# Scoring the level of 32 of a gated recurrence with whole-array matmuls, by turning token blocks of 64 in place of 32

## The chip, the cores and the metric

The kernel runs on one core of a Trainium2 chip. The metric is the device time of one execution in microseconds (us), as a median of several runs. The engines are named as in the profile: PE is TensorE (its matmuls; PEld are its weight loads), DVE is VectorE, ACT is ScalarE, POOL is GpSimd and SP is SyncE.

## The reference

One decoder layer over 2,048 tokens of width 1,024, all in float32. The tokens are normalized and projected; four heads run an HGRN2 recurrence with a forget gate `f` per key channel, eight heads run sliding-window attention with sinks; both are projected back and added. A gated MLP with a short causal convolution and a last normalization follow. The change touches the recurrence, which the reference computes in chunks:

```python
b = jnp.cumsum(gi, axis=2)                                  # gi = log f
rel = b[:, :, :, None, :] - b[:, :, None, :, :]
decay = jnp.exp(jnp.where(causal, rel, -jnp.inf))
scores = jnp.einsum('bhtk,bhsk,bhtsk->bhts', qi, ki, decay)
intra = jnp.einsum('bhts,bhsv->bhtv', scores, vi)
inter = jnp.einsum('bhtk,bhkv->bhtv', qi * jnp.exp(b), state)
```

A score of query t against key s is a sum over 128 channels of q, k and the product of all gates between s and t. This product differs by channel, so the scores are not one plain matmul of q and k.

## The kernel before, in words

The sequence is worked in two halves of 1,024 tokens (`HALF`), each first through the mixer (`hgrn`, `attend`), then through `out_proj`, `gate_up` and `down`. Large products are made in a split form: every operand is a high and a low part (`hi`, `lo`, `XH`, `XL`), and three matmuls take the place of one. The four recurrence heads and four attention units of a half are generators; the list `ORDER` says in which order their stages are traced (`l3`, for example, is the stage of head 3 that holds the levels). The framework then plans every engine's order of instructions with a simulated timeline, so the order on the chip is an interleaving: between a level and the next one of a head, TensorE is given matmuls of other units (`pvv` of L630 to L632, `pop`, `q`, `g` of L218). Each engine runs its own list in order. The last head of a half has the first units of `out_proj` (`pop`) as its company; their operands `XL` are made by VectorE at L230.

The recurrence (`hgrn`) holds `K` and `Q` with the 128 key channels on the partitions and the 1,024 tokens in columns, eight chunks of 128 (`TT` = 8). It scores in levels m = 1, 2, 4, ..., 64 (`LEVELS`). At level m a chunk is cut into blocks of 2m tokens; the queries of the later half of each block are scored against the keys of its earlier half, an m x m tile of `ST` (keys on rows, queries in columns). Afterwards the later half's `Q` is multiplied by the gates' product over the earlier half and the earlier half's `K` by that over the later half (`F`, L523 and L524 or L534 and L535), and `F` is contracted to half its length (L538). So at each level the decay between a block's halves is already in `K` and `Q`.

Levels below 32 take two chunks at a time, u of the first 512 tokens and u + 4 of the second. To make that possible, the tokens of the second 512 are laid out in turned order within blocks of 32: the host permutes the columns of `xP` by `index ^ 31`, and `blocks(t, turn)` reads such columns backwards where true order is needed (L352, L374, L500, L607, L609). In a turned block the earlier half stands behind the later one. Thus the keys wanted from chunk u lie in the even blocks of m, those from chunk u + 4 in the odd ones. ScalarE gathers both into `G` (L515), 128 columns for each u; one matmul for each u (L517) has them as weights and the 2 x 64 queries as moving operand. Four such matmuls make 128 x 128 products each, of which the wanted tiles are a part; VectorE copies these into `ST` with `copy_predicated` under a mask `lmask` (L542). The masks are made by GpSimd in `constants` (L110 to L120).

Levels 32 and 64 are scored in plain slices: for 32, two blocks in each of eight chunks, 16 matmuls (L531) with 32 columns as weights and 32 moving columns; for 64, eight matmuls of 64 columns. ScalarE copies their products from PSUM to `ST`, for 32 in two copies (L552), for 64 in two (L548). The level products `plev` stand in a PSUM ring `hg` of two banks. A float32 matmul has two records in the trace, with a weight load for each.

Later stages read `ST` (L590), the final `K` (L564) and `Q` (L592).

Of the kernel before, what the change touches and what calls it, by code (L numbers as in the profile page):

```python
# [17 lines left out]
P = 128  # L18
D = 1024
KT = D // P  # L20
S = 2048
HALF = 1024
NH = S // HALF
TT = HALF // P
# [17 lines left out]
LEVELS = [1, 2, 4, 8, 16, 32, 64]  # L42
# [7 lines left out]
def hymba_layer(ctx: ExitStack, tc: tile.TileContext, a: dict, out: bass.AP, rows_out: bass.AP):  # L50
    nc = tc.nc
# [47 lines left out]
    def constants():  # L99

        C.own = cp.tile([P, P], F32, name="own")
        C.ownT = cp.tile([P, P], F32, name="ownT")
        C.prevT = cp.tile([P, P], F32, name="prevT")
        for t, op, sgn in ((C.own, ALU.is_ge, 1), (C.ownT, ALU.is_ge, -1), (C.prevT, ALU.is_gt, 1)):
            nc.gpsimd.memset(t, 1.0)
            nc.gpsimd.affine_select(out=t, in_=t, compare_op=op, fill=0.0, base=0,
                                    pattern=[[-sgn, P]], channel_multiplier=sgn)

        C.lmask = {}
        for m in LEVELS[:5]:  # L110
            t = cp.tile([P, 2, 64], F32, name=f"lmask{m}")
            nb = 64 // m
            nc.gpsimd.memset(t, 1.0)
            for side in range(2):
                ts = t[:, side]
                nc.gpsimd.affine_select(out=ts, in_=ts, compare_op=ALU.is_ge, fill=0.0, base=-side * m,
                                        pattern=[[-2 * m, nb], [0, m]], channel_multiplier=1)
                nc.gpsimd.affine_select(out=ts, in_=ts, compare_op=ALU.is_ge, fill=0.0, base=m - 1 + side * m,
                                        pattern=[[2 * m, nb], [0, m]], channel_multiplier=-1)
            C.lmask[m] = t  # L120

        battn = C.battn = cp.tile([P, 6], F32, name="battn")
        nc.sync.dma_start(battn, a["b_attn"])
        C.bq = cp.tile([P, ATT_J], F32, name="bq")
        nc.vector.tensor_scalar(C.bq, battn[:, 0:ATT_J], 0.125, None, op0=ALU.mult)
        C.hgw = cp.tile([P, 1], F32, name="hgw")
        nc.sync.dma_start(C.hgw, a["hg_norm_w"])
        nc.vector.tensor_scalar(C.hgw, C.hgw, 0.5, None, op0=ALU.mult)
        C.sinkb = cp.tile([P, ATT_J, 2], F32, name="sinkb")
        nc.sync.dma_start(C.sinkb.rearrange("p j k -> p (j k)"), a["sinks"].to_broadcast([P, 8]))  # L130
        C.nfw = cp.tile([P, KT], F32, name="nfw")
        nc.sync.dma_start(C.nfw, a["norm_ffn_w"])
        C.fnw = cp.tile([P, KT], F32, name="fnw")
        nc.sync.dma_start(C.fnw, a["final_norm_w"])
        C.cw = cp.tile([P, FT, 4], F32, name="cw")
        nc.sync.dma_start(C.cw, a["conv"])

        lbl = cp.tile([P, 2, HG], F32, name="lbl")
        nc.sync.dma_start(lbl, a["lb_logits"])
        lbm = cp.tile([P, HG], F32, name="lbm")  # L140
        nc.vector.tensor_tensor(lbm, lbl[:, 0], lbl[:, 1], op=ALU.max)
        lbe = cp.tile([P, 2, HG], F32, name="lbe")
        nc.vector.tensor_tensor(lbe, lbl, lbm.unsqueeze(1).to_broadcast([P, 2, HG]), op=ALU.subtract)
        nc.scalar.activation(lbe, lbe, AF.Exp)
        nc.vector.tensor_tensor(lbm, lbe[:, 0], lbe[:, 1], op=ALU.add)
        nc.vector.reciprocal(lbm, lbm)
        C.lb = cp.tile([P, HG], F32, name="lb")
        nc.vector.tensor_tensor(C.lb, lbe[:, 0], lbm, op=ALU.mult)
        C.omlb = cp.tile([P, HG], F32, name="omlb")
        nc.vector.tensor_scalar(C.omlb, C.lb, -0.5, 0.5, op0=ALU.mult, op1=ALU.add)  # L150
        nc.vector.tensor_scalar(C.lb, C.lb, 0.5, 0.5, op0=ALU.mult, op1=ALU.add)
# [172 lines left out]

    def blocks(t, turn=False):

        v = t.rearrange("p (g r) -> p g r", r=32)
        return v[:, :, ::-1] if turn else v

    def across(t, base, dims):  # L330
# [4 lines left out]
    def rows(kv):  # L335
        return slice(kv * HD, (kv + 1) * HD)
# [123 lines left out]
    def hgrn(hf, h, X, invb, vs, WG, gates, mix, p, fu=None):  # L460
# [13 lines left out]
        K = p.tile([P, HALF], F32, tag="K", name="K", bufs=2)  # L474
        nc.vector.tensor_scalar(K, f, -1.0, 1.0, op0=ALU.mult, op1=ALU.add)
        Q = p.tile([P, HALF], F32, tag="Q", name="Q", bufs=2)
# [3 lines left out]
        ST = p.tile([P, TT, P], F32, tag="t4", name="ST", bufs=2)  # L480
# [6 lines left out]
        for k in range(2):  # L487
            r = rows(k)
# [19 lines left out]
        for m in LEVELS:  # L508
            nb = HALF // (2 * m)
            pl = ps("hg", "plev")  # L510
            if m < 32:
                n, nu = 64 // m, TT // 2
                far, near = [[512 - m, 2], [P, nu], [2 * m, n], [1, m]], [[512 + m, 2], [P, nu], [2 * m, n], [1, m]]
                G = p.tile([P, 512], F32, tag="G", name="G", bufs=2)
                nc.scalar.copy(across(G, 0, [[m, 2], [P, nu], [2 * m, n], [1, m]]), across(K, 0, near))  # L515
                for u in range(nu):
                    marks[m] = nc.tensor.matmul(across(pl, u * 64, [[256, 2], [1, 64]]), G[:, u * P:(u + 1) * P],  # L517
                                                across(Q, u * P + m, [far[0]] + far[2:]), start=True, stop=True)
                nf = P // m
                Kv, Qv = across(K, 0, near), across(Q, m, far)  # L520
                Fk = across(F, 1, [[4 * nf - 1, 2], [nf, nu], [2, n], [0, m]])
                Fq = across(F, 0, [[4 * nf + 1, 2], [nf, nu], [2, n], [0, m]])
                nc.vector.tensor_tensor(Kv, Kv, Fk, op=ALU.mult)  # L523
                nc.vector.tensor_tensor(Qv, Qv, Fq, op=ALU.mult)  # L524
            else:
                Qv = Q.rearrange("p (b w m) -> p b w m", w=2, m=m)
                Kv = K.rearrange("p (b w m) -> p b w m", w=2, m=m)
                for c in range(TT):
                    for s0 in range(0, P, 2 * m):
                        o = pl[s0:s0 + m, c * m:(c + 1) * m] if m < 64 else pl[rows(c % 2), c // 2 * m:(c // 2 + 1) * m]  # L530
                        nc.tensor.matmul(o, K[:, c * P + s0:c * P + s0 + m],  # L531
                                         Q[:, c * P + s0 + m:c * P + s0 + 2 * m], start=True, stop=True)
                Fv = F.rearrange("p (b w) -> p b w", w=2)
                nc.vector.tensor_tensor(Qv[:, :, 1], Qv[:, :, 1], Fv[:, :, 0:1].to_broadcast([P, nb, m]), op=ALU.mult)  # L534
                nc.vector.tensor_tensor(Kv[:, :, 0], Kv[:, :, 0], Fv[:, :, 1:2].to_broadcast([P, nb, m]), op=ALU.mult)  # L535
            Fv = F.rearrange("p (b w) -> p b w", w=2)
            Fn = p.tile([P, max(nb, 16)], F32, tag=f"F{m}", name=f"F{m}", bufs=1)[:, 0:nb]
            nc.vector.tensor_tensor(Fn, Fv[:, :, 0], Fv[:, :, 1], op=ALU.mult)  # L538
            F = Fn
            if m < 32:  # L540
                mk = C.lmask[m].bitcast(U32).rearrange("p s t -> p (s t)")
                nc.vector.copy_predicated(across(ST.rearrange("p c t -> p (c t)"), m, far),  # L542
                                          across(mk, 0, [[64, 2], [0, nu], [m, n], [1, m]]),
                                          pl.rearrange("p (s u b m) -> p s u b m", s=2, u=nu, m=m))
                continue
            if m == 64:
                for k in range(2):
                    nc.scalar.copy(ST[0:m].rearrange("p (c k) t -> p c k t", k=2)[:, :, k, m:],  # L548
                                   pl[rows(k), 0:TT // 2 * m].rearrange("p (c m) -> p c m", m=m))
                continue  # L550
            for s0 in range(0, P, 2 * m):
                nc.scalar.copy(ST[s0:s0 + m, :, s0 + m:s0 + 2 * m],  # L552
                               pl[s0:s0 + m, 0:TT * m].rearrange("p (c m) -> p c m", c=TT))
        yield
        v = vs[h]

# [2 lines left out]
        for b in range(NB):  # L559
            pk = ps("hg", "pkn")  # L560
            n = min(4, kept - 4 * b)
            for i in range(n):
                c = slice((b * 4 + i) * P, (b * 4 + i + 1) * P)
# [17 lines left out]
        g = q  # L581
# [3 lines left out]
        for c in range(TT):  # L585
            cs = slice(c * P, (c + 1) * P)
            prev = state[:, h] if c == 0 else SS[:, c - 1]
            o = po[c // 4][:, c % 4 * P:(c % 4 + 1) * P]
# [512 lines left out]
    for hf in range(NH):  # L1101
        X, kv, invb, rs, f0 = nxt
        with ExitStack() as st:
            p = pool(f"mix{hf}", stack=st, reuse_waits="tile")
# [21 lines left out]
        with ExitStack() as st:  # L1126
            p = pool(f"ffn{hf}", stack=st, reuse_waits="tile")
# [5 lines left out]
def _layout(i):  # L1133
# [3 lines left out]
    def cols(w, idx):  # L1137
# [3 lines left out]
    x = i["x"][0]  # L1141
    w_in = i["w_in"][0]
    ar = np.arange
# [4 lines left out]
    rows = [ar(P) + h * P for h in range(4)]  # L1148
# [3 lines left out]
    conv = np.concatenate([i["conv_w"][0], i["conv_b"]], 0)  # L1152
    d = {
        "xT": x.T.reshape(KT, P, S),
        "xP": x[np.where(ar(S) // 512 % 2, ar(S) ^ 31, ar(S))].T.reshape(KT, P, S),
        "norm_mix_w": i["norm_mix_w"][0].reshape(KT, P).T,
        "w_q": np.stack([cols(w_in, h * P + ar(P)) for h in range(4)]),
        "w_f": np.stack([cols(w_in, 512 + h * P + ar(P)) for h in range(4)]),
# [41 lines left out]
```

## Time and profile before

| | before |
|---|---|
| median of 3 runs | 2150.42 us (2149.98 to 2150.78) |
| the profiled execution | 2150.84 us |
| its span | 2149.1 us |
| PE busy | 2130.8 us |
| DVE busy | 1630.1 us |
| ACT busy | 1020.0 us |

The span runs from the first instruction of the program to the last. Busy time is time in which the engine has an instruction under way; matmuls are pipelined and overlap, so PE's busy time says that work was there, and the steps between starts of matmuls say what it cost. In a row of the timeline, `x8` stands for eight instructions merged into one row, and `[0.62 <-DVE XL L230]` says that the engine had been idle 0.62 us before it, until DVE had done line 230. In the view of who waited for whom the numbers are the total, how often, and the longest.

### The profile page before, as it was taken

The numbers are of one execution on the slowest core, as the hardware profiler recorded it, in microseconds if no ns is written. First come the engines' busy times: TensorE is split into PE (matmuls) and PEld (weight loads), VectorE is DVE, ScalarE is ACT, GpSimd is POOL, SyncE is SP. The second block draws the span as 40 slices with busy tenths as digits, with TensorE's granted clock in tenths as the row PEclk, the third lists the DMA queues.
The fourth block names the chain that finished last, engine by engine and source line by source line (L and its number), as shares of the span: only waits on it lengthen the run. The fifth ranks groups of instructions, "written<-read, shape, count | busy, mean of one in ns | idle before, by whom it ended". The sixth has DMA issues, their size and how long they took to land.

```text
span 2149.1 us, 29229 instructions
## 1 busy us (share of the span) xinstructions
PE 2130.8 (99%) x11271; PEld 1790.8 (83%) x11271; DVE 1630.1 (76%) x2443; ACT 1020.0 (47%) x1818; POOL 19.8 (1%) x45
## 2 busy tenths in 40 slices
PE   8999999999999999999999999999999999999998
PEld 6988988888888888888889889888888888888887
DVE  6576768788887888785765767677988888787765
ACT  5445553564444435345634446535544344444453
POOL 2000000000000000000000000000000000000000
PEclk9999999999999999999999999999999999999999
DMA  4111012423232334974631011124233323259643
GB/s 158 40 30 40 31 30 79 137 65 124 92 123 88 103 118 152 370 251 148 214 138 40 30 31 32 40 75 158 69 103 103 118 84 122 95 183 399 238 147 133
DMA packets 91148, 254.41 MB, mean 118 GB/s; under 512 B 11137, under 2 KB 13953, under 8 KB 91009
## 3 DMA queue, kind: packets, MB, share of 16 engines
q1 hardware_dynamic: 90576, 252.29, 34.9%
q8 instruction: 88, 1.44, 0.3%
q14 instruction: 52, 0.42, 0.1%
q10 hardware_dynamic: 432, 0.27, 0.0%
HBM read 195.37 MB, written 57.15 MB: 117 GB/s over the span
## 4 chain that ended last, share of the span: by engine, by line
PE 93%; DVE 5%; ACT 1%; DMA 1%; issue 1%; SPq 0%; DVEq 0%; ACTq 0%
PE X L765 7%; PE X L763 7%; PE X L764 7%; PE pop L218 6%; PE q L218 4%; PE hq L218 4%; PE f L218 4%; PE Y L764 4%; PE Y L763 4%; PE Y L765 4%; PE pdx L950 3%; PE pdx L951 3%; PE pdx L952 3%; PE g L218 3%; PE pdy L950 3%; PE pdy L952 3%
## 5 line engine op out<-in xcount | busy, mean ns | idle before, releaser
L638 ACT CAST whi<-raw 128x1024 fp32r<-128x1024 f32 x88 | 92.7, 1053 | 115.5 <-PE X L764 71.2
L763 PE MATMUL X<-T,whi 128*128 128x512 f32 x352 | 136.9, 389 | 0.0
L764 PE MATMUL X<-T,whi 128*128 128x512 f32 x352 | 136.9, 389 | 0.0
L765 PE MATMUL X<-T,wlo 128*128 128x512 f32 x352 | 136.9, 389 | 0.0
L834 DVE SCALAR_TENSOR_TENSOR y<-ga,cw,y 128x1024 f32<-128x1024 f32 x88 | 112.5, 1278 | 25.9 <-ACT y L832 25.8
L639 DVE TENSOR_TENSOR wlo<-raw,whi 128x1024 fp32r<-128x1024 f32 x88 | 107.0, 1216 | 4.4 <-ACT whi L638 4.4
L769 ACT COPY u<-X 128x512 f32<-128x512 f32 x88 | 51.5, 585 | 122.1 <-PE X L765 121.9
L199 ACT CAST whi<-raw 128x1024 fp32r<-128x1024 f32 x58 | 60.5, 1048 | 98.5 <-issue 20.6
L639 DVE TENSOR_TENSOR xld<-raw,xhd 128x1024 fp32r<-128x1024 f32 x72 | 81.0, 1130 | 18.9 <-ACT xhd L638 18.6
L638 ACT CAST xhd<-raw 128x1024 fp32r<-128x1024 f32 x72 | 69.8, 978 | 40.2 <-DMA raw<-act0T 14.3
L218 PE MATMUL pop<-XL,whi 128*128 128x512 f32 x256 | 84.2, 392 | 0.9 <-DVE XL L230 0.9
L218 PE MATMUL pop<-XH,wlo 128*128 128x512 f32 x256 | 83.3, 391 | 0.7 <-DVE wlo L200 0.7
L218 PE MATMUL pop<-XH,whi 128*128 128x512 f32 x256 | 83.2, 396 | 0.8 <-ACT XH L229 0.5
L200 DVE TENSOR_TENSOR wlo<-raw,whi 128x1024 fp32r<-128x1024 f32 x58 | 70.4, 1217 | 12.9 <-ACT whi L199 12.9
L764 PEld LDWEIGHTS X<-T,whi 128*128 128x128 f32 x352 | 66.1, 188 | 13.7
L765 PEld LDWEIGHTS X<-T,wlo 128*128 128x128 f32 x352 | 66.1, 188 | 13.7
L763 PEld LDWEIGHTS X<-T,whi 128*128 128x128 f32 x352 | 66.1, 188 | 13.7
L630 PE MATMUL pvv<-whi,XH 128*128 128x256 f32 x256 | 73.0, 286 | 0.0
L631 PE MATMUL pvv<-whi,XL 128*128 128x256 f32 x256 | 72.9, 286 | 0.0
L632 PE MATMUL pvv<-wlo,XH 128*128 128x256 f32 x256 | 72.0, 285 | 0.0
L765 PE MATMUL X<-B,wlo 128*128 128x512 f32 x176 | 68.7, 390 | 0.8 <-DVE wlo L639 0.8
L763 PE MATMUL Z<-B,whi 128*128 128x512 f32 x176 | 68.7, 390 | 0.0
(390 smaller groups left out, 6396.5 us busy)
## 6 DMA issues: line engine op xcount, KB each, us to landing
wr<-in_w_down SPq DMA_DIRECT2D x90, 512.0 KB, 5.7
raw<-in_w_gate SPq DMA_DIRECT2D x44, 512.0 KB, 3.6
raw<-in_w_up SPq DMA_DIRECT2D x44, 512.0 KB, 3.6
raw<-act0T SPq DMA_DIRECT2D x20, 512.0 KB, 6.0
raw<-act1T SPq DMA_DIRECT2D x20, 512.0 KB, 5.5
act0B<-y SPq DMA_DIRECT2D x33, 256.0 KB, 2.3
act1B<-y SPq DMA_DIRECT2D x33, 256.0 KB, 2.4
raw<-in_w_out SPq DMA_DIRECT2D x16, 512.0 KB, 3.6
```

Of the source, the lines that this page charges most:

```text
L218: nc.tensor.matmul(o[b], w, x[:, bs], start=f, stop=l)
L630: nc.tensor.matmul(o[:, 0:256], xh[:, t], hi[:, c], start=kt == 0, stop=False)
L631: nc.tensor.matmul(o[:, 0:256], xl[:, t], hi[:, c], start=False, stop=False)
L632: nc.tensor.matmul(o[:, 0:256], xh[:, t], lo[:, c], start=False, stop=kt == KT - 1)
L638: nc.scalar.copy(h, src)
L639: return (eng or nc.vector).tensor_tensor(l, src, h.bitcast(F32), op=ALU.subtract)
L763: nc.tensor.matmul(o, wh[:, ws], xh, start=i == 0 and not more, stop=False, skip_group_check=more)
L764: nc.tensor.matmul(o, wh[:, ws], xl, start=False, stop=False, skip_group_check=more)
L765: nc.tensor.matmul(o, wl[:, ws], xh, start=False, stop=i == 3, skip_group_check=more)
L834: nc.vector.scalar_tensor_tensor(y, g[:, w:w + HALF], C.cw[:, ft, w:w + 1], y, op0=ALU.mult, op1=ALU.add)
L950: nc.tensor.matmul(o, wh[:, i, c], ah[:, i, cols], start=f, stop=False, skip_group_check=more)
L952: nc.tensor.matmul(o, wl[:, i, c], ah[:, i, cols], start=False, stop=l, skip_group_check=more)
```

## The change

Blocks of 64 are turned in place of 32, on the host and in `blocks`. The level of 32 goes over to the branch of the lower levels: a gather by ScalarE into `G`, four matmuls of 128 x 128, the two multiplications with that branch's access patterns, and a masked copy by VectorE with a sixth mask. The plain branch is left to level 64 alone, and the 16 narrow matmuls and two ScalarE copies of the level of 32 go.

```diff
         C.lmask = {}
-        for m in LEVELS[:5]:
+        for m in LEVELS[:6]:
             t = cp.tile([P, 2, 64], F32, name=f"lmask{m}")
...
-        v = t.rearrange("p (g r) -> p g r", r=32)
+        v = t.rearrange("p (g r) -> p g r", r=64)
         return v[:, :, ::-1] if turn else v
...
-            if m < 32:
+            if m < 64:
                 n, nu = 64 // m, TT // 2
...
                 for c in range(TT):
-                    for s0 in range(0, P, 2 * m):
-                        o = pl[s0:s0 + m, c * m:(c + 1) * m] if m < 64 else pl[rows(c % 2), c // 2 * m:(c // 2 + 1) * m]
-                        nc.tensor.matmul(o, K[:, c * P + s0:c * P + s0 + m],
-                                         Q[:, c * P + s0 + m:c * P + s0 + 2 * m], start=True, stop=True)
+                    o = pl[rows(c % 2), c // 2 * m:(c // 2 + 1) * m]
+                    nc.tensor.matmul(o, K[:, c * P:c * P + m], Q[:, c * P + m:(c + 1) * P], start=True, stop=True)
...
-            if m < 32:
+            if m < 64:
                 mk = C.lmask[m].bitcast(U32).rearrange("p s t -> p (s t)")
...
-            if m == 64:
-                for k in range(2):
-                    nc.scalar.copy(ST[0:m].rearrange("p (c k) t -> p c k t", k=2)[:, :, k, m:],
-                                   pl[rows(k), 0:TT // 2 * m].rearrange("p (c m) -> p c m", m=m))
-                continue
-            for s0 in range(0, P, 2 * m):
-                nc.scalar.copy(ST[s0:s0 + m, :, s0 + m:s0 + 2 * m],
-                               pl[s0:s0 + m, 0:TT * m].rearrange("p (c m) -> p c m", c=TT))
+            for k in range(2):
+                nc.scalar.copy(ST[0:m].rearrange("p (c k) t -> p c k t", k=2)[:, :, k, m:],
+                               pl[rows(k), 0:TT // 2 * m].rearrange("p (c m) -> p c m", m=m))
...
-        "xP": x[np.where(ar(S) // 512 % 2, ar(S) ^ 31, ar(S))].T.reshape(KT, P, S),
+        "xP": x[np.where(ar(S) // 512 % 2, ar(S) ^ 63, ar(S))].T.reshape(KT, P, S),
```

## Prediction

> **What bounds the kernel now.** I read the page's busy table and chain first, then TensorE's waits, then the timeline around single levels of the recurrence.
>
> ```profile
> span 2149.1 us, 29229 instructions
> PE 2130.8 (99%) x11271; PEld 1790.8 (83%) x11271; DVE 1630.1 (76%) x2443; ACT 1020.0 (47%) x1818; POOL 19.8 (1%) x45
> PE 93%; DVE 5%; ACT 1%; DMA 1%; issue 1%; SPq 0%; DVEq 0%; ACTq 0%
> ```
> ```profile
> PE kv L218 <- ACT XH L232: 6.0, 1, 6.0
> ...
> PE plev L517 <- DVE Q L524: 0.4, 1, 0.4
> ...
> PE kv L218 <- DVE XL L233: 0.2, 1, 0.2
> ```
>
> TensorE is busy 99% of the span and carries 93% of the chain that ended last. The second fence is the view of who TensorE waited for; it has ten rows, of which the first, one from the middle and the last are shown. They add up to 12.4 us, 6.0 of it at the very first unit. The levels' whole-array matmuls (plev, L517) wait 0.4 us in the whole kernel. So an edit of this recurrence is worth what it changes in TensorE's own time, unless its new steps on VectorE (DVE) or ScalarE (ACT) come so late that TensorE stands. I settle these two things in turn.
>
> **TensorE: 16 narrow matmuls go, 4 whole-array ones come, in each of eight heads** (four heads in each half of the sequence). The level of 16 already has the form that the level of 32 is to get, so one passage of each beside the same neighbours gives the price. In the timeline the columns are start, duration, engine, line; a float32 matmul has two records, so 16 are x32 and 4 are x8.
>
> ```profile
> 82.11 0.28 PE L632 MATMUL pvv<-wlo,XH 128*128 128x256 f32 x1
> 82.23 0.28 PE L630 MATMUL pvv<-whi,XH 128*128 128x256 f32 x1
> 82.24 0.98 PEld L517 LDWEIGHTS plev<-Q,G 128*128 128x128 f32 x8
> 82.36 1.06 PE L517 MATMUL plev<-Q,G 128*128 128x128 f32 x8
> 83.17 0.36 PE L631 MATMUL pvv<-whi,XL 128*128 128x256 f32 x1
> ...
> 86.36 0.28 PE L630 MATMUL pvv<-whi,XH 128*128 128x256 f32 x1
> 86.56 0.59 PEld L531 LDWEIGHTS plev<-Q,K 128*32 128x32 f32 x32
> 86.56 0.70 PE L531 MATMUL plev<-Q,K 128*32 128x32 f32 x32
> 87.19 0.39 PE L631 MATMUL pvv<-whi,XL 128*128 128x256 f32 x1
> ```
>
> Durations overlap, so only starts count. Two pvv matmuls follow each other by 82.23 - 82.11 = 0.12 us. With a whole-array level between them the step is 83.17 - 82.23 = 0.94, so that level costs 0.94 - 0.12 = 0.82 us. With the 16 narrow matmuls the step is 87.19 - 86.36 = 0.83, so the level of 32 costs 0.71 us today. This holds the wait on entry: the first narrow matmul starts 0.20 after its neighbour, against 0.12 to 0.13 for any other. A second passage, beside matmuls of 512 columns:
>
> ```profile
> 178.28 0.39 PE L218 MATMUL g<-XH,wlo 128*128 128x512 f32 x1
> 178.51 0.39 PE L218 MATMUL g<-XH,whi 128*128 128x512 f32 x1
> 178.83 0.70 PE L531 MATMUL plev<-Q,K 128*32 128x32 f32 x32
> 179.46 0.33 PE L399 MATMUL psc<-KS,qh 128*128 128x128 f32 x1
> ```
>
> Here it is 179.46 - 178.51 less the step of 0.23, or 0.72. The narrow matmuls are cheap because they run 0.59 / 32 = 0.018 us apart, where the wide ones run 0.98 / 8 = 0.12 apart. So a quarter as many matmuls are not a gain: the change adds 0.82 - 0.715, about 0.1 us, in each head. For the six heads whose levels lie in gapless TensorE work that is +0.6 us; the last head of each half I treat below.
>
> Why are the wide ones no faster? A 128x128 record and a 128x256 one both follow the one before by 0.12, half the columns for the same time, so their columns do not set the pace. The Trainium skill, "TensorE: Matmul & The Clock Gate", section "LDWEIGHTS (loading the stationary operand)", puts a load at its columns divided by 1.2 GHz. By it both forms load the same 1,024 columns (32 x 32 or 8 x 128), 0.85 us, and the change would be worth 0.0 on TensorE where the rows give +0.1 a head; the wide loads (0.98 us for eight) fit it roughly, the narrow ones (0.59 for 32) beat it, so I keep the rows.
>
> **VectorE gets a masked copy, ScalarE trades two copies for one.** The columns of a line's view are the shortest, median and longest duration in ns; the last row is of the view by groups.
>
> ```profile
> L542 DVE COPY_PREDICATED ST<-lmask,plev x40: 693/718/1341, 64.7 to 1416.7; 128x512 f32<-128x512 uint32 x40
> L515 ACT COPY G<-K x40: 606/622/697, 54.4 to 1408.7; 128x512 f32<-128x512 f32 x40
> L552 ACT COPY ST<-plev x16: 344/362/367, 87.3 to 1419.8; 32x256 f32<-32x256 f32 x16
> L118 POOL TENSOR_SCALAR_AFFINE_SELECT lmask<-lmask 128x64 f32<-128x64 f32 x10 | 7.9, 827 | 0.0
> ```
>
> ScalarE loses 2 x 0.36 and gains 0.62 a head: -0.1 us on an engine that is busy 47% of the time. VectorE gains one copy of 0.72 a head. The mask costs GpSimd one memset and four selects, two of them of this row, about 3 us at the start of the kernel; the first masked copy of all is at 64.7 us, so nothing waits. The turning of 64 tokens changes the stride of copies and products, and no counts. The host's permutation of x adds no DMA.
>
> Is VectorE's copy covered? Two stretches, first head and last head of the first half; the columns are length, then TensorE, weight loads, VectorE and ScalarE busy:
>
> ```profile
> 60.00:95.00 35.00, 35.00 (x325) 33.02 (x324) 18.92 (x29) 14.00 (x31) 0.00 (x0) 1.00 0.08 29
> 320.00:355.00 35.00, 33.88 (x250) 28.35 (x251) 34.86 (x52) 18.02 (x40) 0.00 (x0) 1.00 0.37 116
> ```
>
> In the first head VectorE idles 16 of 35 us and TensorE never: covered. In the last head VectorE is full (34.86 of 35) and TensorE misses 1.1 us: here an added 0.72 us would count, if it stands ahead of what TensorE waits for. The order of that stretch, VectorE first:
>
> ```profile
> 347.39 0.67 DVE L523 TENSOR_TENSOR K<-K,F 128x512 f32<-128x512 f32 x1
> ...
> 351.27 1.21 DVE L230 TENSOR_TENSOR XL<-hg,XH 128x1024 fp32r<-128x1024 f32 x1
> 352.40 0.69 DVE L534 TENSOR_TENSOR Q<-Q,F 128x512 f32<-128x512 f32 x1
> ...
> 358.95 0.69 DVE L534 TENSOR_TENSOR Q<-Q,F 128x512 f32<-128x512 f32 x1 [3.68 <-PE plev L531]
> ```
> ```profile
> 351.22 0.70 PE L531 MATMUL plev<-Q,K 128*32 128x32 f32 x32
> 352.54 0.73 PE L218 MATMUL pop<-XL,whi 128*128 128x512 f32 x2 [0.62 <-DVE XL L230]
> ...
> 1418.56 0.73 PE L218 MATMUL pop<-XL,whi 128*128 128x512 f32 x2 [0.31 <-DVE XL L230]
> ```
> ```profile
> 348.50 0.59 ACT L456 CAST XH<-poT 128x512 fp32r<-128x512 f32 x1 [5.05 <-PE poT L446]
> ```
>
> The multiplications themselves go over to the lower levels' access pattern (L523, 0.67 us, where L534 takes 0.69): no cost shows. TensorE waits for the split XL (L230), which starts at 351.27. The new masked copy can't run before the level's matmuls have ended, and they only start at 351.22, when XL is about to begin. So it comes behind XL, beside the multiplications at 352.40, and behind those VectorE is idle 3.68 us before the level of 64: covered. The new gather G needs K of the level of 16, done at 348.06; ScalarE has been idle for 5.05 us at 348.50, so it can gather then, and at most delays the cast there by 0.2. The level's longer TensorE time falls into the wait for XL. So these two heads cost between 0 and 0.8 each (0.1 + 0.72 if the copy did go first); I take 0.05, near the covered end, because the rows put XL ahead. What is late next there is XL itself, unchanged.
>
> Sum: 6 x 0.1 + 2 x 0.05 = +0.7 us on TensorE's path. The profiled execution took 2150.84 us (span 2149.1 and 1.7 around it), 0.4 over the median of 2150.42; the same step on the median gives 2151.1.
>
> **What the sum can't see: the order is planned anew.** The two halves of the sequence run the same code in slightly different orders.
>
> ```profile
> 1152.02 0.70 PE L531 MATMUL plev<-Q,K 128*32 128x32 f32 x32
> ```
>
> From the level of 32 in the first head to the pop matmul behind it in the last, the first half takes 352.54 - 86.56 = 265.98 us and the second 1418.56 - 1152.02 = 266.54. So a different order moves a half by about 0.6 us; two halves give some 1.2 us about the sum: 2150 to 2152.5.
>
> **The rivals.**
> *VectorE carries the levels (slower).* The copy sits on VectorE between a level and the next one's products in all heads, and TensorE stands for it each time: 8 x 0.72 = 5.8 for the copies and 8 x 0.1 for the matmuls: 2150.42 + 6.6 = 2157.0. For it: the full stretch at 320. Against it: the slack of 16 us in the first head and TensorE's 0.4 us of waits at L517. It decides from the point at which VectorE's queue is longer than the other matmuls set between two levels, which today is so in the last heads alone; a plan that spreads such filler differently could make it so elsewhere. Chance 0.12.
> *The new order drops waits (faster).* K's multiplication waits for the gather alone, where it waited for 16 matmuls; K then runs ahead. All waits but the first in the view of waits are 12.4 - 6.0 = 6.4 us; should a plan happen to lose them all, the time is 2150.42 + 0.8 - 6.4 = 2144.8; losing the two XL waits alone gives 2150.2. Most of the 6.4 lies in other stages, which the change doesn't touch. Chance 0.10, of which 0.05 by more than 4.3 us.
> *Wide matmuls at the pace of their columns.* A step of 0.23 for 512 columns is 0.057 for 128; eight would cost 0.46 where 16 narrow ones cost 0.71: -0.25 x 8 = -2.0, 2148.4. For it: nothing but that row. Against it: the eight records of the level of 16, 0.12 apart, the very form that is to come. Chance 0.03. The Trainium skill, same page, section "Back-to-back issue gap", gives 60 cycles for up to 64 columns and 134 for 128; at 2.4 GHz 32 records would take 0.80 us and 8 would take 0.45, an estimate of -0.35 a head and 2147.6 in all; the trace disagrees at both ends.
>
> **How the numbers follow.** About 0.2% (4.3 us) is what a measurement of this kernel can tell from no change. The forecast of 2151.1 has chance 0.75, and its own range, 2150 to 2152.5, lies inside that. Slower by more: the first rival, 0.12. Faster by more: 0.05. The rest, 0.83, is no change. For 8 in 10 I take the forecast's range, the loss of a few waits and the wide-column case below (2148), and above it the cost of both last heads' copies, the gather behind other ScalarE work and part of the first rival: 2155.
>
> **What would show it right or wrong.** Right: L531 has a third of its 384 records (128), L517 has 384, L542 and L515 have 48, L552's two copies are gone; the step around the level of 32 is 0.94 between pvv matmuls; VectorE's busy time is up by some 5 us and TensorE's by about 1; TensorE's waits stay near 12 us. Wrong: TensorE waits at L517 of a microsecond and more, or at XL in the last heads by over 1; an XL split behind the masked copy; wide records closer than 0.11 us.

## The result, and the profile after

| | before | after |
|---|---|---|
| median | 2150.22 us (2149.43 to 2151.00) | 2154.59 us (2153.93 to 2155.12) |
| the profiled execution | 2150.84 us | 2154.80 us |
| its span | 2149.1 us | 2153.1 us |

The ratio is 1.0020, 95% interval 1.0013 to 1.0027: the change costs 4.4 us where 0.7 were forecast. The time lies near the upper end of the predicted range, and the size is off by a factor of six.

The page of the changed kernel, the lines that answer to the first fence of the prediction:

```profile
span 2153.1 us, 28850 instructions
PE 2133.0 (99%) x11079; PEld 1794.6 (83%) x11079; DVE 1634.5 (76%) x2451; ACT 1019.2 (47%) x1810; POOL 23.3 (1%) x50
PE 94%; DVE 5%; DMA 1%; issue 1%; ACT 0%; SPq 0%; DVEq 0%; ACTq 0%
```

The bound is where it was. The work is what the diff says, too: in the rows by line, with the shortest, median and longest duration in ns, the old L531 is L530 and holds the level of 64 alone, and the level of 32 has moved to L517, L540 and L515.

```profile
L530 PE MATMUL plev<-Q,K x128: 222/222/270, 90.6 to 1427.7; 128*64 128x64 f32 x128
L517 PE MATMUL plev<-Q,G x384: 270/275/382, 61.6 to 1422.0; 128*128 128x128 f32 x192
L540 DVE COPY_PREDICATED ST<-lmask,plev x48: 703/726/1342, 64.6 to 1422.9; 128x512 f32<-128x512 uint32 x48
L515 ACT COPY G<-K x48: 602/622/712, 54.3 to 1416.8; 128x512 f32<-128x512 f32 x48
```

TensorE's timeline around the level of 32 in the first head:

```profile
86.28 0.28 PE L623 MATMUL pvv<-whi,XH 128*128 128x256 f32 x1
86.40 1.06 PE L517 MATMUL plev<-Q,G 128*128 128x128 f32 x8
87.21 0.36 PE L624 MATMUL pvv<-whi,XL 128*128 128x256 f32 x1
```

The step between the two pvv matmuls is 87.21 - 86.28 = 0.93, where the prediction had 0.94; before, it was 0.83. So the price of the wide matmuls was read rightly. What is new stands in the view of who TensorE waited for (total, times, longest):

```profile
PE kv L218 <- ACT XH L232: 6.0, 1, 6.0
PE pop L218 <- DVE wlo L200: 2.0, 4, 0.8
PE pop L218 <- DVE XL L230: 1.0, 1, 1.0
PE plev L517 <- ACT sc L421: 0.9, 1, 0.9
...
PE X L757 <- DVE T L632: 0.7, 1, 0.7
```

To place the loss I cut the span at matmuls that both traces have: the first `pdiag` of a head (which opens it on TensorE), the first `X` (gate_up begins), the first `pdx` (down begins). Each number is the difference of two starts.

| stretch, us | before | after | difference |
|---|---|---|---|
| start to head 1, first half | 60.63 | 60.56 | -0.07 |
| heads 1 to 3, first half | 259.25 | 259.45 | +0.20 |
| last head to gate_up, first half | 121.30 | 124.21 | +2.91 |
| gate_up, first half | 413.23 | 413.24 | +0.01 |
| down to head 1 of the second half | 271.66 | 270.86 | -0.80 |
| heads 1 to 3, second half | 259.38 | 259.37 | -0.01 |
| last head to gate_up, second half | 121.53 | 122.77 | +1.24 |
| gate_up, second half | 413.26 | 414.23 | +0.97 |
| down and end | 228.89 | 228.38 | -0.51 |

The -0.80 is not a gain of the change: a kernel with before's order and work (`turn_only`, below) has 270.90 there. Nor does the -0.51 lie in work that the change touches: it comes behind TensorE's last matmul. The loss lies in the two last heads and in the second gate_up. The first of them, engine by engine. TensorE:

```profile
350.87 1.13 PE L517 MATMUL plev<-Q,G 128*128 128x128 f32 x8 [0.29 <-DVE Q L524]
352.88 1.13 PE L517 MATMUL plev<-Q,G 128*128 128x128 f32 x8 [0.88 <-ACT sc L421]
354.22 1.20 PE L218 MATMUL pop<-XH,whi 128*128 128x512 f32 x4 [0.21 <-ACT XH L229]
355.34 0.69 PE L530 MATMUL plev<-Q,K 128*64 128x64 f32 x16
357.07 0.74 PE L218 MATMUL pop<-XL,whi 128*128 128x512 f32 x2 [1.04 <-DVE XL L230]
```

ScalarE, where eight exponentials of attention (L421, 0.4 us each) and the gather now run ahead of the two casts:

```profile
349.04 0.40 ACT L421 ACTIVATE sc<-sc,m 128x128 f32<-128x128 f32 x1 [0.48 <-DVE m L417]
...
350.98 0.60 ACT L515 COPY G<-K 128x512 f32<-128x512 f32 x1
...
352.66 0.56 ACT L456 CAST XH<-poT 128x512 fp32r<-128x512 f32 x1
353.12 1.04 ACT L229 CAST XH<-hg 128x1024 fp32r<-128x1024 f32 x1
```

VectorE, where the masked copy of the level of 32 stands ahead of the XL split:

```profile
352.04 0.69 DVE L524 TENSOR_TENSOR Q<-Q,F 128x512 f32<-128x512 f32 x1 [0.69 <-PE plev L517]
...
354.52 0.68 DVE L524 TENSOR_TENSOR Q<-Q,F 128x512 f32<-128x512 f32 x1
355.12 0.72 DVE L540 COPY_PREDICATED ST<-lmask,plev 128x512 f32<-128x512 uint32 x1
...
355.84 1.17 DVE L230 TENSOR_TENSOR XL<-hg,XH 128x1024 fp32r<-128x1024 f32 x1
```

Before, the cast L456 began at 348.50 and XL at 351.27. Now the casts begin at 352.66, so no `pop` matmul is ready to stand between the levels of 16 (350.87) and 32 (352.88). The level of 32 needs the Q product of 352.04, which needs the level of 16: TensorE waits 0.88. The view names ScalarE's L421 for it, but the rows show Q ending at 352.73, just ahead. XL comes 4.6 us later than before, and TensorE waits 1.04 for it. Of what runs ahead of the casts and of XL here, only the gather (0.60) and the masked copy (0.72) are the change's own; the rest is the order in which each engine's list was laid out.

### The profile page after: what moved, and what is told of

Read it like the earlier page. It is cut to its first block, busy times and chain, and to the rows that moved or that the text cites. A ratio compares the mean times of both kernels' runs of the same rounds, so it can differ in the third digit from the quotient of the medians.

```text
span 2153.1 us, 28850 instructions
## 1 busy us (share of the span) xinstructions
PE 2133.0 (99%) x11079; PEld 1794.6 (83%) x11079; DVE 1634.5 (76%) x2451; ACT 1019.2 (47%) x1810; POOL 23.3 (1%) x50
## 4 chain that ended last, share of the span: by engine, by line
PE 94%; DVE 5%; DMA 1%; issue 1%; ACT 0%; SPq 0%; DVEq 0%; ACTq 0%
PE X L758 7%; PE X L757 7%; PE X L756 7%; PE pop L218 6%; PE q L218 4%; PE hq L218 4%; PE f L218 4%; PE Y L756 4%; PE Y L758 4%; PE Y L757 4%; PE pdx L945 3%; PE pdx L943 3%; PE pdx L944 3%; PE g L218 3%; PE pdy L945 3%; PE pdy L944 3%
## 5 line engine op out<-in xcount | busy, mean ns | idle before, releaser
L632 DVE TENSOR_TENSOR wlo<-raw,whi 128x1024 fp32r<-128x1024 f32 x88 | 107.4, 1220 | 4.4 <-ACT whi L631 4.4
L632 DVE TENSOR_TENSOR xld<-raw,xhd 128x1024 fp32r<-128x1024 f32 x72 | 81.2, 1133 | 19.8 <-ACT xhd L631 19.3
L757 PE MATMUL X<-T,Sh 128*128 128x512 f32 x176 | 68.6, 390 | 0.7 <-DVE T L632 0.7
```

What stands on the lines that cost most here:

```text
L632: return (eng or nc.vector).tensor_tensor(l, src, h.bitcast(F32), op=ALU.subtract)
L757: nc.tensor.matmul(o, wh[:, ws], xl, start=False, stop=False, skip_group_check=more)
```

## The experiments

Three theories. **P, the plan:** the change's own work costs what the prediction summed, 0.6 to 0.8 us, and the rest are waits of the order that the framework laid out anew. **V:** the added masked copy on VectorE, or else something that belongs to the change itself, costs the time. **T:** the turned strides cost it.

**1. Turning alone** (`turn_only`: before, with blocks of 64 turned; the level of 32 is then scored in the second 512 tokens with the halves of a block exchanged, so part of its products are others than the reference's).

```diff
-        v = t.rearrange("p (g r) -> p g r", r=32)
+        v = t.rearrange("p (g r) -> p g r", r=64)
...
-        "xP": x[np.where(ar(S) // 512 % 2, ar(S) ^ 31, ar(S))].T.reshape(KT, P, S),
+        "xP": x[np.where(ar(S) // 512 % 2, ar(S) ^ 63, ar(S))].T.reshape(KT, P, S),
```

> The kernel before with the turning of 64 alone; the level of 32 keeps its 16 narrow matmuls and scores the second 512 tokens with the block's halves the wrong way round. Every engine's order is that of before, only strides differ. Theory P (the change's own work costs 0.6 to 0.8 us, the other 3.6 us are waits in the order that was planned anew) and theory V (the added masked copy on VectorE costs it): no difference, 2150.2 within 0.5. Theory T (turned strides of 64 cost time): a part of the 4.4 us appears here, 2151.5 to 2154.6.

Measured: 2150.71 us, ratio 1.0000 (0.9991 to 1.0009), every engine's order the same as before's. T falls.

**2. The masked copy taken off VectorE** (`act_tiles`: the changed kernel, level 32 copied out by ScalarE).

```diff
+                if m == 32:
+                    plv = pl.rearrange("p (s u t) -> p s u t", s=2, u=nu)
+                    for s in range(2):
+                        for b in range(2):
+                            r = slice(b * 64 + s * m, b * 64 + s * m + m)
+                            t0 = b * 64 + (1 - s) * m
+                            nc.scalar.copy(ST[r, s * nu:(s + 1) * nu, t0:t0 + m], plv[r, s, :, b * m:(b + 1) * m])
+                    continue
```

> The changed kernel, whose level of 32 is copied out of PSUM by four small ScalarE copies in place of the masked copy on VectorE. V: the loss goes with the copy, 2151 (0.8 over before). P: in the first half's last head the eight exponentials again stand ahead of the cast XH on ScalarE, as in the changed kernel, so most of the loss stays: 2153 to 2155.

Measured: 2154.03 us, 1.0016 (1.0007 to 1.0025). All eight masked copies of the level are gone, and most of the loss stays: 0.6 us less than the changed kernel, within the intervals. In the trace the first half's last head takes 123.61, 0.60 less than in the changed kernel, and TensorE's longest wait for that XL is 0.4 where it was 1.0. V in its first form falls: the copies on VectorE are at most a small part of the loss.

**3. The masked copy moved behind all levels** (`late_copy`: the changed kernel).

```diff
+                if m == 32:
+                    def late_copy(pl=pl, m=m, mk=mk, far=far, n=n, nu=nu):
+                        nc.vector.copy_predicated(across(ST.rearrange("p c t -> p (c t)"), m, far),
...
+                    continue
...
+        late_copy()
```

> The changed kernel with the masked copy of the level of 32 moved behind all levels, so that it can't stand between XL and the products of the levels. V: without the copy ahead of XL the time falls to 2151 to 2152. P: the order is another one again (exponentials behind XH in the first half's last head, ahead of it in the second's), one good half and one bad one: about 2153.

Measured: 2156.16 us, 1.0026 (1.0017 to 1.0035), slower yet; both theories missed. Moving the copy in the source re-planned everything: the first half's last head lost only 0.7 us over before, but heads 1 to 3 of the second half took 253.05 and its last head 131.23, together 3.4 more than before, and the second gate_up 1.1 more. Such an edit does not isolate its own effect.

**4. A re-plan with nothing added** (`swap_before`: before, with two independent products traded in the source at levels 32 and 64).

```diff
-                nc.vector.tensor_tensor(Qv[:, :, 1], Qv[:, :, 1], Fv[:, :, 0:1].to_broadcast([P, nb, m]), op=ALU.mult)
                 nc.vector.tensor_tensor(Kv[:, :, 0], Kv[:, :, 0], Fv[:, :, 1:2].to_broadcast([P, nb, m]), op=ALU.mult)
+                nc.vector.tensor_tensor(Qv[:, :, 1], Qv[:, :, 1], Fv[:, :, 0:1].to_broadcast([P, nb, m]), op=ALU.mult)
```

> The kernel before with two lines exchanged: in the levels of 32 and 64 K is multiplied ahead of Q. No instruction is added or changes its size. V: nothing added, 2150.2. P: the order is planned anew and puts the exponentials ahead of XH in the second half's last head and XL behind other VectorE work in both, so it is slower by 1 to 3 us without any new work: 2151.2 to 2153.2.

Measured: 2156.90 us, 1.0029 (1.0017 to 1.0040), with the same instructions as before. TensorE's waits in its trace:

```profile
PE kv L218 <- ACT XH L232: 5.9, 1, 5.9
PE poT L446 <- DVE pp L438: 2.4, 1, 2.4
PE plev L531 <- DVE den L424: 1.5, 1, 1.5
```

The second and third rows are new and lie in the last heads. The second is a wait of attention (`poT`) in the second half. The third is the level of 64 in the first half:

```profile
353.54 0.70 PE L531 MATMUL plev<-Q,K 128*32 128x32 f32 x32 [0.92 <-DVE Q L524]
355.72 0.98 PE L531 MATMUL plev<-Q,K 128*64 128x64 f32 x16 [1.49 <-DVE den L424]
```

It follows the level of 32 with no other matmul between, so TensorE stands while VectorE makes the two traded products (354.28 to 355.57); the `den` that the view names is the step behind them. Behind this wait the matmuls ran at half the clock for 3.41 us (last section), so the 6.4 us are waits and a slower clock. An order alone can cost more than the whole change did. P's direction holds; its size (1 to 3 us) was too small.

**5. The changed kernel in before's order** (`pinned`). Since any edit draws a new plan, the order itself was held: dependencies that cost no semaphore tie each instruction to the one that stood ahead of it on its engine in the kernel before. The four wide matmuls stand where the sixteen were, the masked copy behind the products of its level; only the new gathers are left to the planner.

```diff
+    no_wait = mybir.DependencyInfo(mybir.DependencyClass.NoSync, mybir.DependencyReason.DATA)
...
+            if last is not None:
+                tc.add_manual_dep(made_ins[i], last.name, no_wait, reason="order of before")
+            last = made_ins[i]
```

> The changed kernel, complete, with the instructions of every engine held to the order that the kernel before has (a list of orders is added to the program; the four wide matmuls stand where the sixteen narrow ones stood, the masked copy directly behind the products of its level). Theory P (the change's own work costs 0.6 to 0.8 us on TensorE, the rest of the 4.4 us are waits of the order planned anew): 2150.8 to 2151.6 us, ratio at most 1.0006, and the first half's last head has the waits of before, no wait of 1 us at XL. Theory V (the added masked copies on VectorE, or something else that belongs to the change itself, cost the time): 2153.5 to 2155, as the changed kernel.

Measured: 2149.56 us, 0.9996 (0.9987 to 1.0005). The 4.4 us are gone, with all of the change's work in place; the time is even 1.2 us below the range that P gave. VectorE in the first half's last head (line numbers are 68 higher here):

```profile
351.08 1.21 DVE L298 TENSOR_TENSOR XL<-hg,XH 128x1024 fp32r<-128x1024 f32 x1
352.21 0.69 DVE L592 TENSOR_TENSOR Q<-Q,F 128x512 f32<-128x512 f32 x1
352.81 0.69 DVE L591 TENSOR_TENSOR K<-K,F 128x512 f32<-128x512 f32 x1
353.42 0.73 DVE L608 COPY_PREDICATED ST<-lmask,plev 128x512 f32<-128x512 uint32 x1
```

This is the place that the prediction gave the copy: behind XL and the products, and TensorE does not stand for it. Heads 1 to 3 take 259.52 and 259.62, against 259.25 and 259.38 before: +0.27 and +0.24, or 0.08 to 0.09 a head. The last heads take 121.25 and 121.55, -0.05 and +0.02. So the change's own work costs 0.5 us in the heads. (`turn_only`, with before's order and work, repeats before's heads within 0.04.) The median shows no such cost: this trace is also shorter in three places where TensorE has none of the change's work. It is 0.46 shorter up to the first head, a stretch that differs by 1.3 among all these traces; 0.79 ahead of the second half, as in `turn_only`; and 0.65 behind TensorE's last matmul. There every kernel with the change is 0.5 to 0.7 shorter than before, and none without it by more than 0.2; why was not tried.

**6. One swap in the held order** (`pinned_copyfirst`: level 32's products and masked copy ahead of XL in both last heads; a different list, the same code).

> The held order with one difference in each half: in the last head VectorE does the two products and the masked copy of level 32 ahead of XL's 1.2 us, as the changed kernel's own plan did in its first half. Theory P: each half's wait of TensorE for XL grows by 0.7 to 1.7 us, 1.5 to 3.5 us over the held order, so 2152.3 to 2155. Theory V (the copy's place is not what counts): within 0.5 us of the held order.

Measured: 2159.06 us, 1.0038 (1.0025 to 1.0050): 9.5 us over the held order, where P had expected 1.5 to 3.5. The five executions run from 2157.24 to 2160.06; the profiled one took 2157.27, and its two last heads hold 7.5 us of the difference (125.73 and 124.60). VectorE and TensorE:

```profile
352.50 0.69 DVE L592 TENSOR_TENSOR Q<-Q,F 128x512 f32<-128x512 f32 x1 [0.99 <-PE plev L585]
...
353.71 0.71 DVE L608 COPY_PREDICATED ST<-lmask,plev 128x512 f32<-128x512 uint32 x1
354.32 1.21 DVE L298 TENSOR_TENSOR XL<-hg,XH 128x1024 fp32r<-128x1024 f32 x1
```
```profile
351.41 1.05 PE L585 MATMUL plev<-Q,G 128*128 128x128 f32 x8
355.58 1.22 PE L286 MATMUL pop<-XL,whi 128*128 128x512 f32 x2 [3.12 <-DVE XL L298]
```

XL starts 2.9 us behind the start of the level's matmuls (354.32 - 351.41), where the held order has it beside them (351.08 against 351.10): 1.8 us are the three steps put ahead of it, and for 1.0 VectorE itself waits for those matmuls, a time that XL filled. TensorE waits 3.1 us in each half (the view has 6.2 us in two), and behind the first of these waits its matmuls ran at half pace (last section). No other place that was tried is as sensitive.

**7. Before's work in the changed kernel's order** (`order_of_after`; the reverse of 5, with the same edit and another list).

> The kernel before, complete and with its own sixteen narrow matmuls and ScalarE copies at level 32, with its instructions held to the order of the changed kernel (level 32's product of K alone comes 3 to 15 VectorE instructions later, since the narrow matmuls still read what it overwrites; the copies of level 32 are free). Theory P: it costs what the changed kernel costs less its own work on TensorE, 2152.8 to 2154.2 us. Theory V: nothing of the change's work is in it, so 2150 to 2151.

Measured: 2153.69 us, 1.0014 (1.0005 to 1.0023). The order alone, with none of the change's work, costs 2.9 us, as P expected; its last heads take 123.62 and 122.79, against 121.30 and 121.53 before. The two medians (-1.2 for the work alone, +2.9 for the order alone) do not add up to 4.4. Each ratio's interval is some 2 us to either side, and the traces show two things that need both: the masked copy ahead of XL, 0.6 us in the first last head (124.21 against 123.62, as in 2), and the second gate_up's 0.97, which is not in this kernel (413.27).

**8. The changed kernel with products traded** (`swap_after`: the edit of 4 made of the changed kernel).

> The changed kernel with the products of Q and K traded in the source at levels 32 and 64, which computes the same with the same instructions and lets the order be planned anew once more; the same edit made of the kernel before cost that one 6.4 us. Theory P: the time moves by 0.5 to 6 us, either way, since a plan is a draw. Theory V: within 0.5 us of the changed kernel, 2154 to 2155.

Measured: 2155.57 us, 1.0023 (1.0014 to 1.0031), 1.0 over the changed kernel, or 0.4 when each is taken against the kernel before that was timed beside it; here the two theories' ranges lie close and the shift is small, so by itself it decides little. The stretches moved far more than the sum: the second half's heads 1 to 3 took 253.54 and its last head 128.74.

**9 to 12. Where in the order it lies.** The held order, with the changed kernel's own order in one part: from the first half's last head to its gate_up (`mix_l1`), the same of the second half (`mix_l2`), everywhere else (`mix_rest`), or as `mix_l1` for VectorE and ScalarE alone (`l1_vector_scalar`). Only the list differs.

> The changed kernel, complete, held to the order of before everywhere but in one stretch: from the first half's last head to its first gate_up matmul every engine keeps the order of the changed kernel's own plan. Held throughout it took 2149.6 us. Theory P, placed (the waits lie in the last heads): in the changed kernel's trace this stretch lengthens by 2.9 us, so 2152.5, between 2151.8 and 2153.2. Rival (the loss is spread over all heads, and a stretch by itself costs next to nothing): 2149.5 to 2150.4.

> The same for the second half's last head alone. Theory P, placed: that stretch lengthens by 1.2 us in the changed kernel's trace, so 2150.8, between 2150.2 and 2151.6. Rival (spread over all heads): 2149.5 to 2150.2.

> The complement: both last heads in the order of before, all else in the order of the changed kernel's own plan. Theory P, placed: the six other heads cost nothing, and the wait of 0.67 us at the second half's gate_up, with what follows it, may stay: 2149.6 to 2150.8. Rival (spread over all heads): 2152 to 2154.

> As the first of these, but in that stretch only VectorE and ScalarE keep the order of the changed kernel's plan, and TensorE, SP and GpSimd that of before. If what costs is that ScalarE runs the eight exponentials ahead of the casts and VectorE the masked copy ahead of XL: at least 2 of the 2.9 us come, 2151.6 to 2153.5. If it is TensorE's own order (levels 16 and 32 directly behind each other): 2149.5 to 2150.6.

| | median, us | ratio | last head, first half | last head, second half |
|---|---|---|---|---|
| pinned | 2149.56 | 0.9996 (0.9987 to 1.0005) | 121.25 | 121.55 |
| mix_l1 | 2152.33 | 1.0007 (0.9998 to 1.0016) | 123.97 | 121.47 |
| mix_l2 | 2150.69 | 0.9999 (0.9991 to 1.0008) | 121.26 | 122.68 |
| mix_rest | 2152.02 | 1.0005 (0.9996 to 1.0014) | 121.59 | 122.21 |
| l1_vector_scalar | 2158.80 | 1.0035 (1.0022 to 1.0047) | 130.71 | 121.54 |

The first two came as expected: 2.8 and 1.1 us over the held order, and in each trace only the stretch given the new order is longer (by 2.7 and 1.1). TensorE's waits in `mix_l1` are those of the changed kernel:

```profile
PE pop L286 <- DVE XL L298: 1.1, 1, 1.1
PE plev L585 <- ACT sc L489: 0.9, 1, 0.9
```

`mix_rest` missed: 2.5 us where at most 1.2 were expected, and 2152.02 just lies in the range of the rival that spreads the loss over all heads (2152 to 2154). Its trace has no wait above 0.6 us behind the first unit, and the loss lies in small pieces: 0.4 at the start, 0.4 and 0.7 in heads 1 to 3, 0.3 and 0.7 in last heads that have before's order. In the changed kernel itself heads 1 to 3 are no longer than in the held order (259.45 and 259.37), so the loss that was to be explained is not spread that way. I take it that the seams between two orders cost this, but no run shows it. So the parts do not add up: 2.8 + 1.1 + 2.5 = 6.4, against 5.0 between the two whole kernels (5.6 when each is taken against the kernel before that was timed beside it).

`l1_vector_scalar` has its loss on the side that was expected of VectorE and ScalarE, and three times the size. TensorE:

```profile
354.25 2.07 PE L286 MATMUL pop<-XH,whi 128*128 128x512 f32 x4 [2.87 <-ACT XH L297]
...
360.61 1.22 PE L286 MATMUL pop<-XL,whi 128*128 128x512 f32 x2 [2.58 <-DVE XL L298]
```

In before's order TensorE wants the `pop` matmul of XH between the levels of 16 and 32. With the casts behind the exponentials it stands there for 2.87 us, then for 2.58 at XL, and from within the first wait on the clock is at half (last section). With the changed kernel's own TensorE order as well, levels 16 and 32 directly behind each other, the stretch is 6.7 us shorter (`mix_l1`). So that order makes the loss of a late XH smaller; that it costs nothing by itself is not shown, since no run has it alone.

The best version of all is `pinned`. It is not measurably faster than the kernel before.

## Why the prediction was right and wrong

- **TensorE's price, right.** +0.1 us a head was forecast; the held order has 0.08 to 0.09 over three heads in each half. The step around the level is 0.93, and the wide records do stand 0.11 apart, so the rival of column pace fails, and with it the estimate of -0.35 a head.
- **The last heads' copy, right in before's order.** It was put behind XL and the products, and priced at 0.05 a head. The held order has it there, at -0.05 and +0.02. The row that put XL ahead was a fact of one plan, though, and the changed kernel's first half has the copy ahead of XL.
- **The gather in ScalarE's idle time, right in the held order only.** "At most delays the cast there by 0.2" did not hold in the changed kernel, where the cast begins 4.2 us later, 0.6 of it for the gather and most of the rest for the exponentials.
- **Rival "VectorE carries the levels", wrong.** It gave 2157.0 and lay nearer to the result than the forecast, but by another mechanism: taking the copies off VectorE returned 0.6 us of 4.4.
- **The step that failed:** "a different order moves a half by about 0.6 us; two halves give some 1.2 us about the sum". The mechanism was named and mis-sized. The two halves of one plan come out of the same planning of nearly the same code, so their difference is no sample of what a new plan does. Five kernels with a new plan (the change, `act_tiles`, `late_copy`, `swap_before`, `swap_after`) stand 3.5 to 6.4 us above the kernel before, none below it. They are fewer than five draws: four hold the change, and `act_tiles` has nearly the changed kernel's order (its stretches differ by at most 0.6 us). I do not know why none fell. The sum of the change's own work, forecast as 0.7, is 0.5 in the heads.
- **The range held in part by luck.** Its upper end, 2155, was made of both last heads' copies, the gather behind other ScalarE work and a part of the rival. The copy ahead of XL did come, but in one last head and for 0.6 us, and the gather beside eight exponentials that the forecast had not counted. Most of the 4.4 us is order, for which the forecast had 1.2.
- **A sum that was wrong:** the ten rows of TensorE's waits add up to 10.7 us, not 12.4. Behind the first row there were thus 4.7 us to lose, not 6.4, and the rival "drops waits" would have given 2146.5, not 2144.8; it fails either way. In the changed kernel the view's rows add up to 13.2. By the forecast's 12 that looks like the sign of being right; against the true 10.7 it is 2.5 us more.
- **What would show it wrong** came true, and named the place: an XL split behind the masked copy, a wait at XL in a last head of just over 1 us (1.04), and 1.2 us of waits at L517 (0.88 and 0.29).

What stays open: the wait of 0.67 us at the second half's gate_up (`X` for `T`, L632), with 0.97 us of the loss. Its order was kept in `mix_rest` and gate_up took 413.26 there, so it is not the order of that stretch by itself. The trace leads it back to a transfer, in rows of ScalarE, VectorE and TensorE:

```profile
1504.23 0.72 ACT L684 ACTIVATE h<-h,nfw 128x512 f32<-128x512 f32 x1 [0.42 <-DMA keep<-h]
1504.98 0.69 DVE L695 TENSOR_TENSOR h<-h,h 128x512 f32<-128x512 f32 x1 [1.81 <-ACT h L684]
1523.11 0.51 PE L757 MATMUL X<-T,Sh 128*128 128x512 f32 x1 [0.67 <-DVE T L632]
```

ScalarE may only overwrite `h` when it has been written out (`keep`, L683). In this trace the second of two such transfers landed 3.28 us after its issue began; before and in `pinned` it took 2.1. VectorE waits 1.81 for ScalarE, against 0.61 before, is 1.2 us late from there on, and is still 0.96 late when it makes `T`. The three other kernels with the change and a plan of their own (`act_tiles`, `late_copy`, `swap_after`) have the same late landing (3.40 to 3.78) and a wait there of 0.8 to 1.2; no other trace has either. What made the transfer late is not shown. And what in the planning puts the exponentials ahead of the casts was not tried.

## What to carry to other kernels

Where a framework lays out the order anew with every edit, price the edit's own work and the new order apart, and size the second by a neutral edit (two independent operations traded), not by the spread inside one plan. Then run the new work in the old order and the old work in the new: the one says what the edit costs by itself, the other how much its order does. Look first at the stretch where the side engines are full; there a 1.2 us step moved behind 2 us of other steps cost 3 us and more.

## What the runs showed of the hardware that was not expected

A wait of TensorE can cost more than its length. In `pinned_copyfirst`, windows of TensorE behind the wait of 3.12 us (length, busy, weight loads, granted clock, then the DMA share and GB/s):

```profile
355.60:358.60 3.00, 3.00 (x7) 2.42 (x8) 0.50 0.55 169
359.00:362.00 3.00, 3.00 (x14) 2.50 (x14) 1.00 0.00 0
```

Matmuls of 512 columns stepped 0.427 us for some 3.3 us, then 0.227 again: 1.4 us lost on top of the wait. It did not happen behind the second wait of 3.12 in `pinned_copyfirst`, nor behind waits of 1.9 in `late_copy` and 2.4 in `swap_before`.

The granted clock shows what decided. In these traces the times between its changes are whole multiples of 3.413 us: 3.41 (twice) and 10.24 at half, 341.33, 344.75, 1792.00, 1795.41 and 2136.74 at full. So I cut TensorE's time at those bounds. The columns are length, TensorE busy, granted clock, DMA share and GB/s; the first two fences are `pinned_copyfirst` around its two waits, the third is `swap_before`.

```profile
352.18:355.59 3.41, 0.29 (x4) 1.00 0.00 0
355.59:359.00 3.41, 3.41 (x8) 0.50 0.50 156
```
```profile
1420.55:1423.97 3.42, 1.98 (x12) 1.00 0.00 0
1423.97:1427.38 3.41, 1.73 (x8) 1.00 0.20 29
```
```profile
352.52:355.93 3.41, 1.00 (x40) 1.00 0.00 0
355.93:359.34 3.41, 3.41 (x24) 0.50 0.05 8
```

The first wait of 3.12 us lies in one stretch of 3.41, and the next stretch has half the clock. The second, just as long, is cut into 1.44 and 1.68 by a bound, and the clock stays. In `swap_before` two waits, of 0.92 and 1.49, share a stretch, 2.4 us idle in all, and the clock drops; its wait of 2.4 in the other half is cut into 1.29 and 1.08. In `l1_vector_scalar` 2.25 us of the wait of 2.87 lie in one stretch; the clock then stays at half for 10.24 us, through the wait of 2.58, and the last head is 9.5 us longer than in the held order. These are the only drops between the start and the last matmul in all fourteen traces, and no other stretch at the full clock has more than 1.68 us idle. So here the idle time within one stretch decided, not the length of a single wait, with a limit between 1.68 and 2.25 us; three drops are few.

The Trainium skill, "TensorE: Matmul & The Clock Gate", section "What's actually happening", has the clock halved after an idle window of some 3.4 us, where the windows run freely. The traces agree on the half clock and on the length of the window; but 2.25 us of idle time within one was enough here, so it need not be idle throughout.

Nor had I expected how far an order alone reaches: 6.4 us from trading two independent products (`swap_before`), 9.5 from moving three steps ahead of one in two places (`pinned_copyfirst`). Both traces hold a drop of the clock.
